# Moving the output stores of a batched matmul two groups nearer to their loads

## The chip, the cores and the metric

The kernel runs on one core of one Trainium2 chip. The metric is device time in microseconds (us). Executions are compared with executions of the kernel before on the same chip and in the same rounds. The ratios compare the runs of the same rounds; they are not quite the ratios of the medians that are quoted. The profile is of one execution: that of the kernel before took 518.98 us, 0.7 us more than its median. A span, from the first to the last instruction, is 1.8 us shorter than the time.

## The reference

```python
b1, b2, m, k, n = 8, 16, 256, 512, 384
x      = randn(b1, b2, m, k)   # float32
weight = randn(b1, b2, k, n)   # float32
out    = np.matmul(x, weight).astype(np.float32)
```

These are 128 independent products of 256x512 by 512x384. All arrays are float32 in memory: 168 MB are read and 50 MB written.

## The kernel before

The kernel takes four products as one group, 32 groups in all. A group has two weight loads of 1.573 MB, one x load of 2.097 MB and one store of 1.573 MB. Each engine has its own list:

- SyncE issues all transfers on one queue. A load waits until the buffer is free again (there are buffers of x for two groups, of weights for two groups, of outputs for four).
- ScalarE casts x to bf16 in four steps, and later copies four results out of PSUM, the buffer that TensorE writes.
- TensorE transposes x in four steps, then multiplies.
- VectorE casts the weights and copies the transposed x from PSUM back to SBUF, the on-chip memory that loads fill and stores read.

The part that matters is SyncE's list. Cuts are marked by three dots.

```python
LAG = 4
...
def load(e, t, U, s):
    n = t * U + s
    for d in range(G // D):
        slot = (s * (G // D) + d) % WS
        if not isinstance(n, int) or n >= 2:
            e.wait_ge(w_cast, n * (G * S) + ((d + 1) * D * S - 2 * G * S))
        e.dma_start(w_sb[slot][:], ...).then_inc(w_in[slot], 16)
    if not isinstance(n, int) or n >= XS:
        e.wait_ge(x_cast, n * T + (1 - XS) * T)
    e.dma_start(x_sb[s % XS][:], ...).then_inc(x_in[s % XS], 16)

def store(e, t, U, s, pieces=1):
    n = t * U + s
    ...
    for q in range(pieces):
        rows = slice(q * R // pieces, (q + 1) * R // pieces)
        e.wait_ge(o_copied, n * T + ((q + 1) * T // pieces + BIAS))
        e.dma_start(out=dram[:, rows], in_=out_sb[s % OS][:, rows]).then_inc(...)
...
def on_sync(e):
    U = OS
    for n in range(LAG):
        load(e, 0, NG, n)
    rounds = (NG - LAG) // U
    with e.Fori(0, rounds) as t:
        for s in range(U):
            load(e, t, U, LAG + s)
            store(e, t, U, s)
    for n in range(rounds * U, NG):
        if n + LAG < NG:
            load(e, 0, NG, n + LAG)
        store(e, 0, NG, n, T if n == NG - 1 else 1)
    ...
```

With LAG = 4 the order at the end is: load 31, then the stores 27, 28, 29, 30, and store 31 in four pieces.

## Time and profile before

| | |
|---|---|
| time, median of the first 3 runs | 518.51 us |
| span of the profiled execution | 517.2 us |
| share of the transfer queue | 99.3% of 16 engines' span |
| busiest compute engine (VectorE) | 64% |
| bytes moved | 218 MB |

The lines of the profile are shown in the prediction below. To read them:

- PE is TensorE (PEld its weight loads), DVE VectorE, ACT ScalarE, POOL GpSimd; SPq is SyncE's list of instructions.
- L103, L111 and L122 are the lines of the kernel that issue a weight load, an x load and a store. L132 casts x, L147 casts the weights, L166 transposes, L180 multiplies, L194 copies out.
- `[4.36 <-DMA x_sb<-in_x_dram]` says that the engine had been idle for 4.36 us and what ended that.
- A stretch gives its length, then the busy time of PE, PEld, DVE, ACT and POOL (with the number of instructions), the granted clock (the share of TensorE's full clock that the chip allowed in that stretch), the busy share of the 16 transfer engines, and GB/s.
- A transfer has landed when its last part has. The compute tail is the time from the landing of the last x to the end of the last copy out.

### The profile page before, as it was taken

The page shows a single profiled execution, that of the slowest core. Times are in us where ns is not written, and L with a number is a line of the kernel's source. Part 1 is how long each engine was busy: PE and PEld are TensorE (multiplying, and loading weights), DVE is VectorE, ACT ScalarE, POOL GpSimd, SP SyncE. Part 2 cuts the span into 40 slices and gives each one's busy share as a digit, 9 for nine tenths or more (in the row PEclk, how much of TensorE's full clock was granted, in tenths as well). Part 3 has the DMA queues.
Part 4 walks back from the last instruction along what each step waited for, and adds up shares of the span by engine and source line. Part 5 has one row for each costly group of instructions (what it writes and reads, how often), then busy time and mean ns, then how long its engine had stood idle before and what let it go on. Part 6 is the DMA issues. An engine that isn't in the chain of part 4 may idle for free.

```text
span 517.2 us, 11523 instructions
## 1 busy us (share of the span) xinstructions
PE 306.6 (59%) x4608; PEld 200.6 (39%) x4608; DVE 332.8 (64%) x384; ACT 236.7 (46%) x264; POOL 0.7 (0%) x6
## 2 busy tenths in 40 slices
PE   0478776556665457645577554776446765467752
PEld 0345444334443334433344332444324443244431
DVE  3698875667556676556675566855658656676550
ACT  0465564443644436435355354454444544544441
POOL 0000000000000000000000000000000000000000
PEclk9998877878777887878777778877788877778777
DMA  8999999999999999999999999999999999999996
GB/s 340 430 423 424 424 432 426 429 428 430 432 427 427 427 428 432 429 427 430 426 431 431 426 429 430 427 432 427 427 429 429 427 433 425 430 428 430 429 428 251
DMA packets 18869, 218.18 MB, mean 422 GB/s; under 512 B 2096, under 2 KB 2096, under 8 KB 2608
## 3 DMA queue, kind: packets, MB, share of 16 engines
q1 hardware_dynamic: 18864, 218.11, 99.3%
q8 instruction: 3, 0.05, 0.0%
q14 instruction: 2, 0.02, 0.0%
HBM read 167.77 MB, written 50.33 MB: 422 GB/s over the span
## 4 chain that ended last, share of the span: by engine, by line
DMA 81%; ACT 10%; PE 4%; issue 3%; ACTq 0%; SPq 0%
DMA x_sb<-in_x_dram 81%; ACT x_bf L132 9%; PE po L180 2%; PE pt L166 1%; ACTq L130 0%; ACT out_sb L194 0%; SPq L111 0%; SPq L103 0%; ACT L132 0%; ACTq L193 0%; SPq L282 0%; SPq L55 0%
## 5 line engine op out<-in xcount | busy, mean ns | idle before, releaser
L147 DVE CAST w_bf<-w_sb 64x1536 bf16<-64x1536 f32 x256 | 244.4, 955 | 47.2 <-DMA w_sb<-in_weight_dram 38.5
L166 PE MATMUL pt<-identity,x_bf 128*128 128x128 f32 x512 | 123.7, 425 | 199.3 <-ACT x_bf L132 199.1
L180 PE MATMUL po<-w_bf,x_t 128*32 128x384 bf16 x4096 | 185.1, 342 | 1.0 <-issue 1.0
L166 PEld LDWEIGHTS pt<-identity,x_bf 128*128 128x128 f32 x512 | 91.8, 216 | 232.1 <-issue 218.3
L194 ACT COPY out_sb<-po 128x768 f32<-128x768 f32 x128 | 102.2, 798 | 147.2 <-PE po L180 147.2
L153 DVE COPY x_t<-pt 128x1024 bf16<-128x1024 bf16 x128 | 88.4, 691 | 122.3 <-PE pt L166 121.8
L132 ACT CAST x_bf<-x_sb 128x1024 bf16<-128x1024 f32 x128 | 124.4, 1042 | 80.9 <-DMA x_sb<-in_x_dram 80.8
L180 PEld LDWEIGHTS po<-w_bf,x_t 128*32 128x32 bf16 x4096 | 108.8, 101 | 73.8 <-issue 14.2
L132 ACT ACT_TABLE_LOAD x8 | 10.3, 1283 | 42.9 <-DMA x_sb<-in_x_dram 42.9
masks.py:199 POOL TENSOR_SCALAR_AFFINE_SELECT identity<-identity 128x128 f32<-128x128 f32 x1 | 0.3, 292 | 0.2 <-POOL identity L200 0.2
L200 POOL MEMSET identity<- 128x128 f32 x1 | 0.2, 204 | 0.5 <-SPq L55 0.5
L271 POOL MEMSET const-bfloat16-1.0<- 128x1 bf16 x1 | 0.1, 101 | 0.0
L271 POOL MEMSET const-uint8-127<- 128x1 uint8 x1 | 0.1, 101 | 0.0
L271 POOL MEMSET const-float32-0.0<- 128x1 f32 x1 | 0.1, 98 | 0.2 <-issue 0.2
L271 POOL MEMSET const-float32-1.0<- 128x1 f32 x1 | 0.1, 98 | 0.0
## 6 DMA issues: line engine op xcount, KB each, us to landing
w_sb<-in_weight_dram SPq DMA_DIRECT2D x64, 1536.0 KB, 27.5
x_sb<-in_x_dram SPq DMA_DIRECT2D x32, 2048.0 KB, 27.5
out_dram<-out_sb SPq DMA_DIRECT2D x31, 1536.0 KB, 30.7
out_dram<-out_sb SPq DMA_DIRECT2D x4, 384.0 KB, 5.9
```

What stands on the lines that cost most here:

```text
L132: e.copy(out=x_bf[s % BS][:, rows], in_=x_sb[s % XS][:, rows].rearrange("p r (q s c) -> p r s q c", s=S, c=KO),).then_inc(x_cast, 1)
L147: e.tensor_copy(out=w_bf[(s * G + d * D + a) % WBS][h * HP : (h + 1) * HP], in_=w_sb[slot][a * HP : (a + 1) * HP, h * KO : (h + 1) * KO, : ...
L153: e.tensor_copy(out=x_t[s % TS][:, 2 * q : 2 * q + 2], in_=pt[(s * T + q) % PT][:].bitcast(bf16),).then_inc(t_copied, 1)
L166: ins = e.transpose(pt[(s * T + q) % PT][:, rr, h, :], words[:, 2 * q + rr, h :: KO // 2], identity[:],)
L180: ins = e.matmul(po[(s * T + q) % PO][mine, rr, :N], x_t[s % TS][:, 2 * q + rr, ko // 2, mine, ko % 2], w_bf[(s * G + i) % WBS][:, ko, :], ...
L194: e.copy(out=out_sb[s % OS][:, 2 * q : 2 * q + 2, :], in_=po[(s * T + q) % PO][:, :, :N],).then_inc(o_copied, 1)
L200: e.memset(identity[:], 0.0).then_inc(id_done, 1)
L271: nc = _bacc.Bacc("TRN2", target_bir_lowering=False, num_devices=1)
```

## The change

Intent: let each store follow its own load more closely, so that fewer stores are left when the last load is in: three instead of five.

```diff
-    LAG = 4
+    LAG = 2
```

The order at the end is now: load 30, store 28, load 31, store 29, store 30, store 31 in four pieces. Only SyncE's list changes.

## The prediction

> **What bounds the kernel now.** I first read the page's slices and its queue table, to see which resource is full:
>
> ```profile
> DMA  8999999999999999999999999999999999999996
> GB/s 340 430 423 424 424 432 426 429 428 430 432 427 427 427 428 432 429 427 430 426 431 431 426 429 430 427 432 427 427 429 429 427 433 425 430 428 430 429 428 251
> q1 hardware_dynamic: 18864, 218.11, 99.3%
> ```
>
> All traffic runs through one queue, the one that SyncE fills. It is full in every slice except the first and the last, at about 428 GB/s. No compute engine is above 64% (DVE). The change moves no bytes: 32 groups of 5.24 MB in (two weight loads of 1.573 MB, one x load of 2.097 MB) and 1.573 MB out stay 218 MB. So the body of the run is set by the queue, and only its two ends, or a hole in the middle, can change the time.
>
> Next, what the issuing engine waits for (total us, times, longest us), and the issues (KB each, us from issue to landing):
>
> ```profile
> SPq L103 <- DVE w_bf L147: 269.5, 60, 8.6
> SPq L111 <- ACT x_bf L132: 122.5, 30, 5.6
> SPq L122 <- ACT out_sb L194: 35.5, 6, 16.2
> ...
> w_sb<-in_weight_dram SPq DMA_DIRECT2D x64, 1536.0 KB, 27.5
> x_sb<-in_x_dram SPq DMA_DIRECT2D x32, 2048.0 KB, 27.5
> out_dram<-out_sb SPq DMA_DIRECT2D x31, 1536.0 KB, 30.7
> ```
>
> SyncE waits for input buffers (L103, L111), hardly ever for a finished output tile (L122: 6 times, all near the end). A load lands 27.5 us after its issue, which is 1.7 times the 16.0 us that a group takes (below): more than a group of work always stands in the queue, which is the slack against holes.
>
> Then the end, from the chain of work and the ordered list of instructions (start us, length us):
>
> ```profile
> 468.88 27.67 DMA x_sb<-in_x_dram
> ...
> 480.68 3.89 ACT L132 CAST x_bf<-x_sb 128x1024 bf16<-128x1024 f32 x4 [4.36 <-DMA x_sb<-in_x_dram]
> ...
> 496.66 3.89 ACT L132 CAST x_bf<-x_sb 128x1024 bf16<-128x1024 f32 x4 [3.83 <-DMA x_sb<-in_x_dram]
> ...
> 503.02 0.80 ACT L194 COPY out_sb<-po 128x768 f32<-128x768 f32 x1 [2.48 <-PE po L180]
> ...
> 506.92 0.80 ACT L194 COPY out_sb<-po 128x768 f32<-128x768 f32 x1 [0.50 <-PE po L180]
> ```
>
> The last x lands at 468.88 + 27.67 = 496.55. From there to the end of the last copy (507.72) is a compute tail of 11.17 us, in which the four last store pieces become ready at 503.82, 505.12, 506.42 and 507.72. The landing before it was 16.0 us earlier: one group's 6.816 MB in 16.0 us is 426 GB/s.
>
> Last, the stretches around the end (us, busy time by engine, granted clock, DMA share, GB/s):
>
> ```profile
> 480.60:496.60 16.00, 10.12 (x144) 6.45 (x144) 10.40 (x12) 7.08 (x8) 0.00 (x0) 0.72 1.01 429
> 496.60:502.00 5.40, 4.17 (x32) 3.22 (x36) 2.48 (x4) 3.89 (x4) 0.00 (x0) 0.58 1.01 428
> 502.00:506.00 4.00, 4.00 (x104) 2.71 (x100) 0.29 (x1) 1.97 (x3) 0.00 (x0) 1.00 1.00 424
> 506.00:511.00 5.00, 0.87 (x24) 0.32 (x12) 0.00 (x0) 1.22 (x2) 0.00 (x0) 1.00 0.99 408
> 511.00:516.00 5.00, 0.00 (x0) 0.00 (x0) 0.00 (x0) 0.00 (x0) 0.00 (x0) 0.54 0.24 96
> ```
>
> The queue stays full through the whole compute tail, until 511. That is the point of the five stores: behind the last load stand stores 27 to 30 (four of 1.573 MB; 4 x 1.573 MB / 426 GB/s = 14.8 us), and the compute tail of 11.2 us hides under them. The final store's first piece is issued at 503.8, some 7.5 us before the slowest engine has done with store 30 (496.55 + 14.8 = 511.3). After 511 only stragglers run (share 0.24); the last piece, issued at 507.72, lands 8.0 us later at 515.7, and the span ends 1.5 us after that. The end of the kernel before is thus pure transfer time; nothing at the end waits for compute.
>
> **What the Trainium skill says.** "DMA: Bandwidth & Descriptors", section "Anatomy of one DMA": semaphore waits are done by the issuing sequencer before dispatch, the DMA engines only drain their queues. So a store's wait at L122 holds back everything that SyncE would issue after it, but nothing already queued. The trace agrees as far as it goes: the waits above are all SyncE's own. The same section puts a fixed cost of about 2 us on a DMA (its fit is for the GpSimd path), mostly the receipt of the last byte. In this trace the first load, on an empty queue, is issued at 0.97 and the first bytes move in the stretch 1.8 to 2.0, so about 1 us goes before the data. Section "Queues, rings and completion order": on each engine descriptors are consumed in ring order, but completion is not first in, first out. The trace shows both: the 16.0 us between two x landings fit the bytes queued between them, and the first final piece lands (503.82 + 6.0 = 509.8) before store 30 does (492.83 + 19.2 = 512.1).
>
> **The change part by part.** Only SyncE's order changes; the other four engines' instruction lists are identical.
>
> Start: two groups instead of four are issued ahead of the loop, but loads 2 and 3 have to wait for the casts of groups 0 and 1 in both versions (two x buffers, weight buffers for two groups). Store 0 now comes before load 3 and waits until group 0 is copied out at 29.8. Load 3's first weight load, issued at 28.3 before, slips by 1.5 us. The queue then holds loads 0 to 2, 3 x 5.24 MB / 428 GB/s = 36.8 us from 2 us on, so it runs till about 39. Cost: 0.
>
> Middle: relative to the landing of x of group n, ACT has cast it at about +4, its last copy out ends at +11.7 (464.59 to 476.32 in group 29), and the first weight half of group n+1 is cast at +11.4 (its landing +7.5 and four casts of about 0.98). In the new order store n (ready +11.7) stands before the load of group n+3, whose first weight load was free to go at +11.4 and so slips by some 0.3 us; its second half and its x (+15.4 and +20) don't slip at all. With over 20 us of work queued that costs 0, and nothing accumulates, since every release time hangs on the landings. A store is issued about 12 us after the landing of its own x and lands behind x of group n+2 (+32 and a store's 3.7): about 24 us from issue to landing instead of 30.7.
>
> End: two more stores (27 and 28) go ahead of the last x. It lands 2 x 1.573 MB / 426 GB/s = 7.4 us later, at 503.9. Behind it stand stores 29 and 30, 7.4 us, until 511.3 on the slowest engine, as before. But the compute tail of 11.2 us also starts 7.4 us later: the pieces are ready at 511.1, 512.4, 513.7 and 515.1 instead of 503.8 to 507.7. So 11.2 us of compute have only 7.4 us of stores above them, and the queue drains to single pieces. Each of these moves 0.393 MB, 0.92 us at 426 GB/s, less than the 1.30 us between them, so the last piece alone counts: ready 515.1, about 1 us to the first byte, 0.9 us of data, about 1 us of receipt (an estimate from the skill's 2 us in all and the 1 us that the trace shows before the data). It lands at 518.1 to 518.3, where it landed at 515.7. Sum: 0 + 0 + 2.6 us, hence 518.5 + 2.6 = **521.1 us**, slower by 0.5%.
>
> **The rivals.** (a) Shorter drain: fewer stores after the last load, two stores less, up to 7.5 us won (511). Against it: the two stores do not vanish, they run earlier in a queue that was already full (share 1.01 in 480.6 to 496.6), so the last load moves back by just what the drain is shortened. It needs an idle queue to fill, and only the first and last slices have any. (b) The L122 wait becomes the bound in the middle: SyncE waits some 7.7 us in each group for the copies (from x cast to copied out). If this emptied the queue by even 1 us in each of 29 groups, the time would be near 550. Against it stand 27.5 us to landing in a 16 us period. A milder form, a total of 2 to 4 us of holes from the start or from slow-clock groups, is possible and would give 523 to 525. (c) The tail is hidden anyway: the slowest engine, which was still working at 515 while most were done by 511, has its backlog of earlier stores in the new order too, so the late pieces cost it little, and the time stays at 518.5 to 519.5. For it: the last piece took 8.0 us to land although it was small. (d) The exposed tail is longer: group 30's tail was 492.83 - 480.57 = 12.3 us at a lower clock, not 11.2, and a piece on an empty queue may take 4 us; together 523.
>
> **Range and chances.** The tail gives 2.6 us; (c) takes up to 2 us off, (d) adds about 2. Executions agree within 0.2 us. Eight times in ten I expect 519.5 to 522.8. 2% is 10.4 us, far above all but rival (b) in its strong form and beyond the full gain of (a). Chances: faster 0.005, within 2% 0.975, slower 0.02.
>
> **What would show it.** Right if: the middle slices keep about 428 GB/s; the L122 wait for the output copies appears in nearly every group, for about 7 us, while the L103 wait shrinks by as much; stores land about 24 us after issue, loads still 27.5; the last x lands near 503.9 and the last copy ends near 515.1; the DMA share falls well under 1 between 511 and 515, and the last piece lands within 4 us of its issue. Wrong if the middle slices drop (b), if the last x still lands near 496.6 (a), or if the last copy ends near 515 but the span grows by less than 1 us (c).

## The result, and the profile after

The changed kernel takes **521.2 us** (median of 6 runs, 521.15 to 521.81), the kernel before 518.29 us in its 6 runs; the ratio is 1.006 (95% interval 1.0047 to 1.0073). So it is slower by 0.6%, far within 2%.

First the slices and the queue of the changed kernel's page:

```profile
DMA  8999999999999999999999999999999999999994
GB/s 348 428 413 407 426 431 429 429 429 427 429 430 425 436 426 428 429 427 430 431 426 430 426 431 430 431 426 428 428 431 430 428 426 430 431 428 430 427 428 196
q1 hardware_dynamic: 18864, 218.11, 99.0%
```

The bytes are the same. The middle is as full as before. The clear difference is in the last slice: 196 GB/s instead of 251. The third and fourth slice are a little lower (413 and 407 instead of 423 and 424); the experiments e2_held and e3_endonly below say what that is worth.

Then SyncE's waits (total us, times, longest us), and the issues (KB each, us to landing):

```profile
SPq L122 <- ACT out_sb L194: 245.1, 35, 16.1
SPq L111 <- ACT x_bf L132: 127.9, 30, 5.6
SPq L103 <- DVE w_bf L147: 62.4, 32, 8.1
...
w_sb<-in_weight_dram SPq DMA_DIRECT2D x64, 1536.0 KB, 26.9
x_sb<-in_x_dram SPq DMA_DIRECT2D x32, 2048.0 KB, 27.6
out_dram<-out_sb SPq DMA_DIRECT2D x31, 1536.0 KB, 23.3
out_dram<-out_sb SPq DMA_DIRECT2D x4, 384.0 KB, 2.3
```

SyncE now waits for the output copies in every group (L122, 35 times, 245 us in all), and by about as much less for the weight casts (L103, 269.5 to 62.4). This looks alarming, but it is an exchange of one wait for another: a load still lands 27 us after its issue, so work always stood in the queue. The last line is new in kind: the final pieces land 2.3 us after their issue, where the last of them took 8.0 us before. They meet an empty queue. (The page's 5.9 us for the pieces before is no time of one piece. The four share one semaphore, and its 64 increments, one for each of 16 parts of four pieces, are dealt out in order of time, 16 to each piece. Where the pieces overlap, only the last one's landing is certain.)

The end, from the chain of work and from the list of instructions in order of time (start us, length us):

```profile
476.54 27.75 DMA x_sb<-in_x_dram
...
504.40 3.89 ACT L132 CAST x_bf<-x_sb 128x1024 bf16<-128x1024 f32 x4 [3.60 <-DMA x_sb<-in_x_dram]
...
510.94 0.80 ACT L194 COPY out_sb<-po 128x768 f32<-128x768 f32 x1 [2.65 <-PE po L180]
...
514.84 0.80 ACT L194 COPY out_sb<-po 128x768 f32<-128x768 f32 x1 [0.50 <-PE po L180]
```

The last x lands at 476.54 + 27.75 = 504.29, 7.7 us later than before. The last copy ends at 515.64. The last piece is issued right after it and lands 2.3 us later, near 518.0; the span ends at 519.4.

The same stretches in the view by windows (us, busy time by engine, granted clock, DMA share, GB/s):

```profile
488.50:504.40 15.90, 10.25 (x144) 6.53 (x144) 10.40 (x12) 7.09 (x9) 0.00 (x0) 0.72 1.01 429
504.40:508.00 3.60, 2.43 (x11) 2.00 (x12) 1.01 (x2) 3.60 (x4) 0.00 (x0) 0.50 0.99 420
508.00:511.00 3.00, 3.00 (x47) 2.00 (x49) 1.75 (x3) 0.35 (x2) 0.00 (x0) 0.79 0.26 107
511.00:512.00 1.00, 1.00 (x32) 0.67 (x24) 0.00 (x0) 0.73 (x1) 0.00 (x0) 1.00 0.00 0
512.00:516.00 4.00, 2.79 (x72) 1.63 (x60) 0.00 (x0) 2.40 (x3) 0.00 (x0) 1.00 0.70 278
```

Between 508 and 512 the transfer engines run dry while TensorE is still transposing and multiplying the last group. Before, the share stayed at 0.99 until 511. This idle stretch is where the time went.

### The profile page after: what moved, and what is told of

Its sections match the earlier page's. It is cut to its first block, busy times and chain, and to the rows that moved or that the text cites. A ratio compares the mean times of both kernels' runs of the same rounds, so it can differ in the third digit from the quotient of the medians. Undisturbed runs are those within 1.5% of the kernel's fastest.

```text
span 519.4 us, 11523 instructions
## 1 busy us (share of the span) xinstructions
PE 306.4 (59%) x4608; PEld 199.8 (38%) x4608; DVE 332.8 (64%) x384; ACT 236.7 (46%) x264; POOL 0.7 (0%) x6
## 4 chain that ended last, share of the span: by engine, by line
DMA 82%; ACT 10%; PE 4%; issue 3%; ACTq 0%; SPq 0%
DMA x_sb<-in_x_dram 82%; ACT x_bf L132 9%; PE po L180 2%; PE pt L166 2%; ACTq L130 0%; SPq L111 0%; ACT out_sb L194 0%; SPq L103 0%; ACTq L193 0%; ACT L132 0%; SPq L282 0%; SPq L55 0%
## 6 DMA issues: line engine op xcount, KB each, us to landing
out_dram<-out_sb SPq DMA_DIRECT2D x31, 1536.0 KB, 23.3
```

## The experiments

All times are medians. "Before" is the kernel before in the same rounds.

| run | stores behind the last load (full + last) | what is different | us | before | ratio |
|---|---|---|---|---|---|
| e1_lag3 | 3 + 1 | LAG = 3 | 518.45 | 518.69 | 0.9993 |
| e2_held | 4 + 1 | LAG = 2, end as with 4 | 518.52 | 518.69 | 0.9999 |
| e3_endonly | 2 + 1 | LAG = 4, end as with 2 | 521.45 | 518.69 | 1.0049 |
| e4_lag1 | 1 + 1 | LAG = 1 | 544.86 | 518.69 | 1.0499 |
| e5_split2 | 2 + 1 | LAG = 2, last x in pieces | 519.35 | 518.19 | 1.0023 |
| e6_split4 | 4 + 1 | LAG = 4, last x in pieces | 518.62 | 518.19 | 1.0007 |
| e7_whole2 | 2 + 1 | LAG = 2, last store whole | 524.37 | 518.19 | 1.0113 |
| e8_whole4 | 4 + 1 | LAG = 4, last store whole | 518.21 | 518.19 | 0.9997 |
| e9_actstore | at most 1 + 1 | stores issued by ScalarE | 527.3 | 518.3 | 1.017 |
| e10_dmaonly | 4 + 1 | transfers alone, wrong | 517.11 | 518.3 | 0.9975 |

The theory: the compute that follows the last x is hidden only as far as full stores stand behind that load; the part not covered is added to the time. The main rival: the store's wait in the middle, or the changed start, costs the time.

### The end alone, and the middle alone

**e2_held** keeps the changed order up to store 26, then issues the loads 29 to 31 first:

```diff
-        rounds = (NG - LAG) // U
+        rounds = (NG - LAG) // U - 1
...
+        for n in range(rounds * U, NG - 5):
+            load(e, 0, NG, n + LAG)
+            store(e, 0, NG, n)
+        for n in range(NG - 5 + LAG, NG):
+            load(e, 0, NG, n)
+        for n in range(NG - 5, NG):
+            store(e, 0, NG, n, T if n == NG - 1 else 1)
```

> The changed kernel (two groups behind, SyncE waiting for the output copies in the middle) with the end alone undone: the loads 29, 30 and 31 go before store 27, so that five stores stand behind the last load. Theory (the cost is the uncovered compute tail at the end): last x lands near 496.9, last copy ends near 508.2, time 518.3 +- 0.6. Rival (the waits in the middle or the start cost it): stays near 521. The part of the 2.9 us that stays is the price of middle and start; the theory expects at most 0.5.

Measured: 518.52 us, ratio 0.9999 (0.9986 to 1.0012). From its waits and its instructions in order of time:

```profile
SPq L122 <- ACT out_sb L194: 221.2, 33, 12.6
...
496.70 3.89 ACT L132 CAST x_bf<-x_sb 128x1024 bf16<-128x1024 f32 x4
...
507.18 0.80 ACT L194 COPY out_sb<-po 128x768 f32<-128x768 f32 x1 [0.50 <-PE po L180]
```

Of the 245 us of waiting for output copies 221 are there, and so is about half of the dip in the third and fourth slice (421 and 413 GB/s), yet the time is that of the kernel before. Start and middle cost nothing that can be measured.

**e3_endonly** is the opposite. It keeps LAG = 4 and only moves the stores 27 and 28 ahead of load 31. Abridged, with the lines that go left out:

```diff
+        store(e, 0, NG, NG - 5)
+        store(e, 0, NG, NG - 4)
+        load(e, 0, NG, NG - 1)
+        for n in range(NG - 3, NG):
+            store(e, 0, NG, n, T if n == NG - 1 else 1)
```

> The kernel before (four groups behind, SyncE never waiting for outputs in the middle) with the end alone changed: stores 27 and 28 go before load 31, three stores stand behind the last load. Theory: last x lands near 504, last copy ends near 515.3, last piece lands 2.3 us after its issue, time 521 +- 0.6. Rival (middle or start): stays at 518.3.

Measured: 521.45 us, ratio 1.0049 (1.0036 to 1.0062). From its chain and its windows:

```profile
468.37 35.94 DMA x_sb<-in_x_dram
...
511.00:512.00 1.00, 1.00 (x32) 0.61 (x24) 0.00 (x0) 0.42 (x1) 0.00 (x0) 1.00 0.00 0
```

The last x lands at 504.31, within 0.02 us of the changed kernel, although this run starts as the kernel before does: so the dip in the third and fourth slice costs nothing by the time the last x lands. The same idle microsecond stands at 511 to 512. The two runs together settle the place: the loss (2.8 us here, 2.9 in the changed kernel) arises in the order of the last few transfers. The last copy ended at 516.28, a microsecond later than expected: in this execution the granted clock stayed at 0.50 until 510, and the tail was 12.0 us.

### How many stores are enough

**e1_lag3**: `LAG = 3`.

> Stores come three groups behind: four stores, three of them full, stand behind the last load. Theory (the compute tail of 11.3 us at the end is hidden only as far as stores stand above it): three stores are 11.1 us, about the tail's length; the last x lands 3.7 us later than in the kernel before (near 500.3 us), the last copy ends near 511.5, the last piece lands near 515 as before; time 518.3 +- 0.6. Rival 'each store less behind the last load costs the same' (linear): 519.7. Rival 'the waits of SyncE for output copies in the middle cost the 2.9 us': they are there with three groups too, or nearly, so about 521.

Measured: 518.45 us, ratio 0.9993 (0.998 to 1.0006). From its chain, its instructions and its windows:

```profile
472.15 27.77 DMA x_sb<-in_x_dram
...
510.56 0.80 ACT L194 COPY out_sb<-po 128x768 f32<-128x768 f32 x1 [0.50 <-PE po L180]
...
508.00:511.00 3.00, 2.50 (x64) 1.34 (x52) 0.00 (x0) 2.00 (x3) 0.00 (x0) 1.00 0.82 327
```

Its last x lands at 472.15 + 27.77 = 499.92 and its last copy ends at 511.36; the last piece lands 4.0 us after its issue, near 515.4, and the share at 508 to 511 is 0.82, where the changed kernel has 0.26. Three full stores, 11.1 us, just about cover a tail of 11.4 us. So the cost is not linear in the number of stores: the step from four full stores to three is free, the step from three to two costs nearly 3 us. One part of the rival's expectation was wrong in its premise: with three groups SyncE waits for output copies only 6 times, as with four, because the cast that load n+3 waits for comes after the copies of group n on ScalarE.

**e4_lag1**: `LAG = 1`, with the first four rounds written out so that no wait has a value below one.

> Stores one group behind: two stores, one of them full, behind the last load. Theory: at the end 3.7 us more of the compute tail are uncovered: 521.2 + 3.7 = 524.9 if nothing else happens. In the middle a store is issued 11.7 us after its x landed, and then only 4.3 us of load n+1 are left in the queue, which is just enough; but at the start load 2 has to wait behind store 0 until about 30 us, and loads 0 and 1 fill the queue only to some 27 us on most engines, so a hole of 2 to 4 us comes on top there: 527.5 +- 1.5 in all, with the hole to be seen between 26 and 32 us. Rival (middle waits cost per group): over 535.

Measured: 544.86 us (540.1 to 547.22), ratio 1.0499. This is 17 us more than was expected, and the miss is instructive. Its windows and instructions (profiled execution, 543.23 us) in one of the groups that begin ScalarE's loop of four:

```profile
216.81 1.28 ACT L132 ACT_TABLE_LOAD   x1 [6.33 <-DMA x_sb<-in_x_dram]
...
229.24 0.80 ACT L194 COPY out_sb<-po 128x768 f32<-128x768 f32 x1 [0.50 <-PE po L180]
230.21 0.36 SPq L122 DMA_DIRECT2D out_dram<-out_sb  x1
...
228.00:230.00 2.00, 1.18 (x32) 0.50 (x20) 1.94 (x3) 1.50 (x2) 0.00 (x0) 1.00 0.79 336
230.00:232.00 2.00, 0.00 (x0) 0.00 (x0) 1.94 (x3) 0.04 (x1) 0.00 (x0) 0.83 0.54 229
```

Here the store waits until 230.2, SyncE cannot issue the next load before it, and the queue runs low at 228 to 232. The times between successive x landings tell where nearly all of it arose. In the changed kernel every interval from the third on is 15.9 us. With one group it is 21.4 us once at the start (13.98 in the changed kernel), and in nine of the later intervals between 16.6 and 17.9 us, which is 13.2 us more than nine times 15.9. Of the 7.4 us at the start 3.7 are the store that now goes ahead; the hole of 3.7 us was expected. The 13 us in the middle were not. Seven of the nine are the landing two groups after one with a table load of 1.28 us on ScalarE, which lengthens that group's compute tail. My reckoning of "4.3 us left, just enough" was too generous. It took the queue for a single pipe; the engines do not finish together (the last to land of a load's 16 parts was up to 2.8 us behind the first in these groups), the first bytes of a new issue move about 1 us after it (in the kernel before, issue at 0.97, bytes from 1.8 to 2.0), and I had forgotten the table load. Which of these weighs most was not tried.

**e9_actstore** starts from the kernel before and lets ScalarE issue the stores, so that no load is held back by one. The last round of ScalarE's loop is written out. Abridged:

```diff
 # SyncE: loads only
-                store(e, t, U, s)
 # ScalarE, after the four copies of a group
+            if not last:
+                store(e, t, U, s)   # the last group: one piece after each copy
```

> Stores are issued by ScalarE as soon as it has copied a group out; SyncE issues loads alone and never waits for an output. A store then shares the engines with the loads from the moment of its issue, so nearly all stores but the last are gone before the last x lands, as with stores one group behind, but no load is held back. Question: was the large loss with stores one group behind (544.9 us, where 527.5 was expected) due to loads held behind the store's wait? Theory yes: here no holes in the middle (428 GB/s in every middle slice), the last x lands after all 168 MB of loads and some 48 MB of stores, near 510 us, the last copy ends near 521.5, time 526 +- 2. Rival (stores as early as this disturb the loads in themselves): over 535 again, with the middle slices near 410 GB/s.

Measured: 527.3 us, ratio 1.017 (1.0154 to 1.0185). From its chain of work:

```profile
481.63 28.95 DMA x_sb<-in_x_dram
```

The last x lands at 510.58, the last copy ends at 521.70, and the middle slices stand near 429 GB/s. So early stores do not harm the transfers. Most of the loss with one group (17.6 of 26.2 us) is gone where no load stands behind a store's wait. The run also puts the stores on a queue of their own; the two were not tried apart. What remains, 9.0 us, I put down to the tail of 11.1 us, of which little is covered. The landing itself was late too: fifteen of the 16 parts of the last x were in at 506.69, the last came at 510.58, and at 510 to 511 the share of the transfer engines was 0.06.

### Changing the length of the tail

In **e5_split2** and **e6_split4** the last x load is cut into four pieces, each with a semaphore of its own, so that casts and transposes begin earlier (LAG = 2 and LAG = 4). The last round of ScalarE's loop is written out, which drops one of its eight table loads, that of group 28. Abridged:

```diff
+        if isinstance(n, int) and n == NG - 1:
+            for q in range(T):
+                rows = slice(2 * q, 2 * q + 2)
+                e.dma_start(out=x_sb[s % XS][:, rows], in_=dram[:, rows]).then_inc(
+                    x_last[q], 16)
+            return
```

> The changed kernel (two groups behind, three stores behind the last load) with the last x load in four pieces of two rows each, on semaphores of their own, so that casting and transposing begin before the whole x is there. The last piece lands near 504.3 as before, but after it come only one cast, one set of transposes and the matmuls: the compute tail shrinks by three of four steps of about 0.95 us, from 11.35 to some 8.4 us, against 7.4 us of stores above it. Theory (the length of the compute tail sets the end): last copy ends near 512.7, last piece lands near 515, and the drain of the slowest DMA engine is the bound again: time 518.6 +- 0.6. Rival (the order of stores itself costs, not the compute tail): stays at 521.2.

> The kernel before with the last x load in the same four pieces. Theory: its compute tail is hidden under four stores, so a shorter one gains nothing: 518.3 +- 0.4. Rival (its end hangs on compute as well): 2 to 3 us faster, 515.5.

Measured: 519.35 us (ratio 1.0023, 1.0009 to 1.0036) and 518.62 us (1.0007, 0.9993 to 1.0021). Cutting the x load wins back about 1.9 of the 2.9 us lost with two groups and wins nothing with four. That is the theory's pattern, but the first is somewhat above the range expected. From the last cast (504.20) to the end of the last copy (513.78) it took 9.6 us, not 8.4. The matmuls of the last group in e5_split2, from the list of TensorE's instructions:

```profile
506.43 6.49 PE L191 MATMUL po<-w_bf,x_t 128*32 128x384 bf16 x128
```

and in the changed kernel:

```profile
509.40 5.38 PE L180 MATMUL po<-w_bf,x_t 128*32 128x384 bf16 x128
```

They began earlier but met a granted clock of 0.50 until 508 and took 1.1 us longer, which is the missing part (1.1 of the 1.2 us).

In **e7_whole2** and **e8_whole4** the last store is one transfer instead of four pieces (LAG = 2 and LAG = 4):

```diff
-            store(e, 0, NG, n, T if n == NG - 1 else 1)
+            store(e, 0, NG, n)
```

> The changed kernel with the last store as one transfer instead of four pieces. Theory: it is exposed there, the transfer of 1.57 MB is issued at 515.7 on an empty queue and takes 3.7 us of data plus the 1.4 us that a piece needs besides its own 0.9, so it lands near 520.8 instead of 518.0: time 524.0 +- 0.6. Rival (the end is transfer time of the queue anyway): 521.2.

> The kernel before with the last store as one transfer. It is issued at 507.8, and the slowest engine is at earlier stores until about 511.5. Theory (the end is pure queue time): nothing changes on the slowest engine, 518.3 +- 0.5, while the faster engines, which the pieces fed from 503.8 on, now run dry at about 507.5 for some tenths of a us. Rival (the late readiness is felt): 2 us or more slower.

Measured: 524.37 us (ratio 1.0113, 1.0097 to 1.0128; 3.2 us over the changed kernel's 521.2) and 518.21 us (0.9997). The issue-to-landing times of all stores, first e7_whole2:

```profile
DMA to landing us min/median/max: 5.0/23.2/24.3
```

and e8_whole4:

```profile
DMA to landing us min/median/max: 7.7/30.6/33.8
```

The smallest value is the last store. On the empty queue it takes 5.0 us instead of 2.3; these 2.7 us are most of the 3.2 us that were lost. (In the profiled execution, the slowest of the four, the last copy also ended 1.0 us later, at 516.68.) Behind other stores a whole store costs nothing. The four pieces, then, are worth 3 us with two groups and nothing with four.

### The floor

**e10_dmaonly** has the transfers of the kernel before in the same order and no compute. A load waits for the landing of the load that had its buffer, and the stores send zeros.

> Wrong on purpose: the transfers of the kernel before alone, in its order (four groups behind, last store in four pieces), with no compute; a load waits only for the landing of the load that had its buffer, the stores send zeros. Theory (the kernel before is pure transfer time but for its compute start, which does not matter): 517 +- 1.5 us, so the kernel before has no more than about 1 us to gain from anything but the transfers. Rival (5 us are lost at the end of the kernel before to late pieces, as its last slice of 251 GB/s suggests): 513 or less.

Measured: 517.11 us, with a wrong result; ratio 0.9975 (0.9962 to 0.9989). Its last windows:

```profile
506.00:511.00 5.00, 0.00 (x0) 0.00 (x0) 1.00 0.99 409
511.00:515.00 4.00, 0.00 (x0) 0.00 (x0) 1.00 0.29 116
```

They look like those of the kernel before: full until 511, then stragglers. The kernel before is within 1.2 us of its bare transfers in this order, so with this order compute can give back no more than that. Other orders were not run without compute. None of the correct versions beats the kernel before by more than noise.

## Why the prediction was right

It said 521.1 us; 521.2 was measured, and the mechanism was tested part by part. That the two figures agree to 0.1 us is luck: 2.6 us were added to 518.5, the median of three runs, where 2.9 over 518.29 were measured. "Executions agree within 0.2 us" was too tight as well; six runs of each kernel spread over 0.7 to 0.8 us.

- **Start and middle cost 0**: right. e2_held has both and no loss. (Load 3's first weight load slipped by 2.8 us, from 28.32 to 31.15, and not by 1.5; that cost nothing either.) The waits moved from L103 to L122 as described, and stores land 23.3 us after issue, where 24 was said.
- **The last x moves back by two stores**: right. 7.4 us was worked out, the trace shows 504.29 - 496.55 = 7.7.
- **The compute tail is covered for 7.4 us and exposed beyond**: right. The tail was 11.35 us instead of 11.17, the last copy ended at 515.64 instead of 515.1. But "until 511.3" holds for the slowest engine alone (store 30 landed at 511.7; in the kernel before at 512.1). The sign that the prediction named, a share well under 1 between 511 and 515, came three microseconds early: the share was down to 0.26 from 508 on. Nor is the tail less the full stores (4.0 us) what was added. Worked out from these traces, tail and last piece together (11.35 + 2.3 = 13.7 us) stand against all three stores behind the load (11.1 us), which leaves 2.6 us; with three full stores it is 13.7 against 14.8, and nothing is left.
- **The last piece's time**: mis-sized by a little. I reckoned 3.0 to 3.2 us to landing (the parts that I listed add up to 2.9); it took 2.3. By luck this made good the half microsecond by which the copy was late, and the landing near 518.0 is just under the 518.1 to 518.3 worked out. The sum was 2.6 us; the medians differ by 2.9, the two profiled spans by 2.2, because the profiled execution of the kernel before was 0.7 us slower than its median.
- **One reading of the trace failed**: the prediction took the first final piece to land at 509.8 us, before store 30 (512.1), and so to show that a later transfer can complete before an earlier one. The four pieces share one semaphore: 509.84 is its 16th increment of 64, from whichever parts came first, and the parts of store 30 themselves came in between 507.7 and 512.1. Nothing in the sum rests on it.
- **Rival (a), a shorter drain**: fell. The queue was full, so a store that leaves the end pushes the last load back by its own length.
- **Rival (b), the wait in the middle**: fell for two groups, but it is real. It stands one step further on: with one group the middle loses 13 us, and the time is 544.86 us.
- **Rival (c), the slowest engine's backlog hides it**: fell. Store 30 was issued at 500.83 and landed 10.9 us later, at 511.7; the first piece was issued at 511.76. Nothing of the backlog was left to hide under.
- **Rival (d), a longer tail**: the tail hardly grew in this run, and the piece took 2.3 us, not 4. But a clock that stays low can lengthen the tail, as the rival said: the last group's matmuls took 5.3 us in the changed kernel, 5.9 in e3_endonly (clock 0.50 until 510, tail 12.0 us) and 6.4 in e7_whole2 (0.50 until 511, tail 12.5 us).

## What to carry to other kernels

In this kernel, bound by one full transfer queue, moving transfers earlier did not shorten the end; it only changed what stands behind the last load. Where a kernel is bound in the same way, keep enough work there that needs no further compute to cover the compute that follows the last load: here 11.1 us of stores for a tail of 11.4, and more won nothing. Judge a large new wait on the issuing engine by the times from issue to landing and not by its total: with 245 us of such waits loads still landed 27 us after their issue, in a period of 16 us, and nothing was lost; with 435 us (one group) the weight loads landed after 12.9 us, less than a period, and the queue had holes.

## What the Trainium skill lacked or had wrong

- "DMA: Bandwidth & Descriptors", section "Anatomy of one DMA", gives a fixed cost of about 2.0 us, fitted for transfers issued from GpSimd. For stores issued by SyncE on an empty queue these runs show 2.3 us for 0.393 MB and 5.0 us for 1.573 MB from issue to landing. The line through the two has a slope of 437 GB/s and a fixed part of 1.4 us (2.3 - 0.9). The page gives no such fit for SyncE's transfers. Its slope agrees with these two sizes, its fixed part does not; my estimate built on it was 0.6 to 0.9 us too long.
- The same page, in "Latency and other measured facts", tells that two of the engines are usually slower and ties it, as a best guess, to transfers issued from GpSimd; it gives no spread for transfers issued by SyncE. Here all of the kernel's transfers are issued by SyncE, and still the 16 increments of the last x's semaphore came in over 3.4 us in the kernel before: twelve of them at least 2.2 us before the last. The trace does not name the engines, so whether it is these two stays open. Here the queue ran dry on most engines some microseconds before the slowest was done (in the changed kernel from 508, store 30 landing at 511.7).
- No page treats the end of a full queue: that the stores behind the last load hide the compute after it. Here two full stores instead of three cost nearly 3 us (521.2 against 518.45), and four instead of three won nothing.
